# A hybrid attention step: the prompt attention in written order, larger groups of key blocks, and the sample recurrence on VectorE

## The chip, the cores and the metric

The kernel runs on one core of a Trainium2 chip. The metric is the device time of one execution in microseconds (us). A profile is one execution recorded by the hardware profiler. PE is TensorE's matmul, PEld its weight load, DVE is VectorE, ACT ScalarE, POOL GpSimd, SP SyncE, which issues most DMAs. An instruction's line (L1263) is a line of the kernel's source.

## What is computed

One layer of a hybrid decoder: 1024 prompt rows and 8 sample rows (one new row for each of 8 sequences with 1024 past rows) go through one projection, whose columns feed three groups of heads. All is float32. In the code that the change touches:

```python
def masked_softmax(s, mask): ...
# NSA group, 8 query heads on 2 KV heads, head_dim 64, a block of 128 queries at a time
s = jnp.einsum('qghd,cgd->qghc', qg, ck) * SCALE      # compressed blocks
p = masked_softmax(s, valid[:, None, None, :])
o_c = jnp.einsum('qghc,cgd->qghd', p.astype(cv.dtype), cv)
...
ss = jnp.einsum('qghd,qgnsd->qghns', qg, kg) * SCALE  # selected blocks: 16 of 64 rows
...
s = jnp.einsum('qghd,kgd->qghk', qg, kw) * SCALE      # window of 512 rows
...
return g[..., 0:1] * o_c + g[..., 1:2] * o_s + g[..., 2:3] * o_w
...
# RWKV group, one step of the recurrence; the sample rows make one such step
sa = jnp.einsum('bhvk,bhk->bhv', s, -kk_t)
s = s * w_t[:, :, None, :] + sa[..., None] * b_t[:, :, None, :] + v_t[..., None] * k_t[:, :, None, :]
return s, jnp.einsum('bhvk,bhk->bhv', s, r_t)
...
# memory group: 4 heads, softmax over 256 memory rows
s = jnp.einsum('bthd,bmhd->bhtm', q, mkv[:, :, 0]) * SCALE
...
cat = jnp.concatenate([o_nsa.reshape(b, t, NSA_W) * jax.nn.silu(z_nsa),
                       o_rw * jax.nn.silu(z_rw),
                       o_mem.reshape(b, t, MEM_W) * jax.nn.silu(z_mem)], axis=-1)
return cat @ w_out
```

With 1024 prompt rows there are 16 blocks of 64, so the 16 selected ones are all of a query's past.

## The kernel before

The program has three phases. Up to about 545 us come the projections and the prompt's RWKV scan; from 545 to about 915 us the prompt attention (`phase2`); then the sample's attention and the output projection. The change lies in `phase2` and in what runs beside it.

`phase2` walks 8 tiles of 128 queries from the last (i = 7) to the first (i = 0). A tile has four units (i, g, hp): KV head g and a pair hp of query heads. A unit has two branches: b = 0 the selected keys (i + 1 blocks of 128), b = 1 the window (at most five blocks). For each unit:

- `attn_scores` makes the scores p_s in PSUM. Keys are held as a high and a low part, so each stretch of keys is two matmuls (kh, L1263, and kl, L1264), and each masked block of 128 gets a third, a bf16 matmul of an identity with a mask (L1266), right behind its kl. A reduction on DVE gives the row maximum nm (L1279 in tiles 7 to 4, L1288 in 3 to 0), ScalarE takes the exponential (L1280, L1290), DVE makes the gate divided by the sum (fac, L1291 and L1292), and the probabilities p are scaled by it: the selected branch on DVE (L1296), the window on GpSimd (L1298). There are two score buffers.
- `attn_out` transposes p in blocks of 128x128 on PE (`pt_copy`, p_pT, L1236) into one of three PSUM banks, which ScalarE (L1240) and DVE (L1242) copy out in turn, and multiplies the values by the transposed blocks (p_o, L1320), 64 columns of the array a head. It does so in groups of four key blocks, with the next group's transposes written ahead of a group's p_o. The compressed branch comes last (cvk, L1323), then the product with the gate's SiLU into cat (L1325).

The scores of a unit are written LAG = 2 units ahead of its `attn_out`, in pieces between the groups. Beside them two chains of side tasks advance: `tile_tasks` (the next tile's queries in `q_stack`, the compressed branch in `attn_cmp`, the RWKV output in `attn_rwkv`, the memory heads in `attn_mem`) and `sample_tasks` (`sample_setup` with the norms of the sample's queries and keys, its memory and window attention, `sample_rwkv` with the recurrence, and the first gather of cache pages, L1660). How many of their steps run at each group is set by the table RATE, two numbers a tile. Within these, a scheduler orders the instructions of each engine.

`sample_rwkv` keeps the state as 128 partitions x 1024 (16 rows of 64) and makes its step with seven products or sums of 128x1024 on GpSimd (L1932 to L1940), with two reductions on DVE.

`attn_mem` takes the four heads at once: eight matmuls (L1337, L1338) into p_sm of 128x1024, one reduction (L1339), four exponentials (L1341), one product (L1343), eight transposes, sixteen products p_om and the product into cat (L1360).

## Time and profile before

| | us |
|---|---|
| median of 3 runs (1100.33 to 1103.5) | 1102.4 |
| the profiled execution | 1101.94 |
| its span in the trace | 1100.2 |
| PE busy | 1021.0 (93%) |
| DVE busy | 719.2 (65%) |
| ACT busy | 480.6 (44%) |
| POOL busy | 127.7 (12%) |

Shares of the whole span average over stages with different limits. The span is read by stretches: in each the busy time of an engine stands beside the length, and the granted clock shows whether TensorE ran at its upper level (2.4 GHz, 1.00) or partly at the lower one (1.2 GHz, 0.50).

### The profile page before, as it was taken

The page shows a single profiled execution, that of the slowest core. Times are in us where ns is not written, and L with a number is a line of the kernel's source. Part 1 is how long each engine was busy: PE and PEld are TensorE (multiplying, and loading weights), DVE is VectorE, ACT ScalarE, POOL GpSimd, SP SyncE. Part 2 cuts the span into 40 slices and gives each one's busy share as a digit, 9 for nine tenths or more (in the row PEclk, how much of TensorE's full clock was granted, in tenths as well). Part 3 has the DMA queues.
Part 4 walks back from the last instruction along what each step waited for, and adds up shares of the span by engine and source line. Part 5 has one row for each costly group of instructions (what it writes and reads, how often), then busy time and mean ns, then how long its engine had stood idle before and what let it go on. Part 6 is the DMA issues. An engine that isn't in the chain of part 4 may idle for free.

```text
span 1100.2 us, 27501 instructions
## 1 busy us (share of the span) xinstructions
PE 1021.0 (93%) x11419; PEld 830.8 (76%) x11419; DVE 719.2 (65%) x2065; ACT 480.6 (44%) x1056; POOL 127.7 (12%) x161
## 2 busy tenths in 40 slices
PE   6999999889999999999989979999998687999998
PEld 5998788678877787878767767777776576778676
DVE  7667488346925982734488985757788766575562
ACT  7553233324422433234266556665665355425320
POOL 1000000000000000000032231121326511101000
PEclk9999999999999999999999999999999699999999
DMA  8323113213311172361460034322100226526321
GB/s 258 98 56 88 43 44 111 61 41 86 88 51 32 44 183 65 90 179 41 128 195 21 25 117 130 101 59 71 34 4 14 99 57 227 199 88 239 116 77 60
DMA packets 124034, 102.25 MB, mean 93 GB/s; under 512 B 33455, under 2 KB 109646, under 8 KB 121734
## 3 DMA queue, kind: packets, MB, share of 16 engines
q1 hardware_dynamic: 119846, 82.50, 25.9%
q0 software_dynamic: 2304, 16.78, 4.5%
q8 instruction: 90, 1.47, 0.6%
q10 hardware_dynamic: 1760, 1.21, 0.4%
q14 instruction: 34, 0.28, 0.1%
HBM read 81.88 MB, written 22.78 MB: 95 GB/s over the span
## 4 chain that ended last, share of the span: by engine, by line
PE 68%; DVE 18%; DMA 5%; ACT 4%; issue 3%; POOL 1%; SPq 0%; DVEq 0%; ACTq 0%; POOLq 0%
PE p_pr L83 16%; PE p_pr L257 7%; PE p_pT L1236 6%; PE p_o L1320 5%; PE p_out L1996 5%; PE p_s L1263 3%; DMA wor<-in_w_out_dram 2%; PE p_it L83 2%; PE p_s L1264 2%; PE p_hid L958 2%; PE p_z L83 1%; DVE wlo L245 1%; PE p_iy L83 1%; DMA xg<-in_cache_nsa_dram,idx 1%; DVE nm L1279 1%
## 5 line engine op out<-in xcount | busy, mean ns | idle before, releaser
L83 PE MATMUL p_pr<-h,whi 128*128 128x512 f32 (+5 forms) x928 | 233.2, 343 | 0.0
L83 PEld LDWEIGHTS p_pr<-h,whi 128*128 128x128 f32 (+1 forms) x928 | 146.6, 185 | 18.0 <-issue 3.0
L83 PE MATMUL p_pr<-h,wlo 128*128 128x512 f32 (+5 forms) x464 | 152.7, 329 | 0.1
L83 PEld LDWEIGHTS p_pr<-h,wlo 128*128 128x128 f32 (+1 forms) x464 | 85.5, 184 | 9.7
L1263 PE MATMUL p_s<-kh,qs 128*128 128x512 f32 (+3 forms) x192 | 77.4, 404 | 13.4 <-ACT p L1280 8.2
L257 PE MATMUL p_pr<-h,whi 128*128 128x256 f32 (+2 forms) x416 | 87.8, 307 | 0.4 <-ACT whi L244 0.4
L1236 PE MATMUL p_pT<-ident,p 128*128 128x128 f32 x528 | 77.0, 288 | 9.3 <-DVE cat L1360 5.5
L1320 PE MATMUL p_o<-pt,vs 128*64 128x128 f32 x1056 | 84.9, 287 | 0.7 <-DVE cat L1325 0.6
L1298 POOL TENSOR_TENSOR p<-p,fac 128x640 f32<-128x640 f32 (+4 forms) x64 | 62.9, 1003 | 168.6 <-DVE fac L1292 105.7
L1236 PEld LDWEIGHTS p_pT<-ident,p 128*128 128x128 f32 x528 | 60.5, 146 | 20.9 <-issue 6.6
L1320 PEld LDWEIGHTS p_o<-pt,vs 128*64 128x64 f32 x1056 | 61.7, 140 | 15.8 <-issue 12.4
L245 DVE TENSOR_TENSOR wlo<-wraw,whi 128x1024 fp32r<-128x1024 f32 (+1 forms) x35 | 41.8, 1198 | 44.2 <-ACT whi L244 43.6
L1280 ACT ACTIVATE p<-p_s,nm 128x640 f32<-128x640 f32 (+3 forms) x64 | 55.8, 872 | 31.9 <-DVE nm L1279 28.1
L257 PEld LDWEIGHTS p_pr<-h,whi 128*128 128x128 f32 x416 | 66.7, 191 | 3.7 <-ACT whi L244 0.8
L1279 DVE TENSOR_REDUCE nm<-p_s 128x1 f32<-128x640 f32 (+3 forms) x64 | 58.4, 918 | 15.6 <-PE p_s L1266 15.4
L1264 PE MATMUL p_s<-kl,qs 128*128 128x512 f32 (+3 forms) x192 | 65.1, 344 | 0.0
L257 PE MATMUL p_pr<-h,wlo 128*128 128x256 f32 (+2 forms) x208 | 63.0, 305 | 0.0
L1242 DVE COPY pt<-p_pT 128x512 f32<-128x512 f32 (+1 forms) x72 | 47.8, 663 | 20.7 <-PE p_pT L1236 19.3
L1240 ACT ACTIVATE pt<-p_pT 128x512 f32<-128x512 f32 (+1 forms) x72 | 42.4, 591 | 41.9 <-PE p_pT L1236 37.5
L244 ACT ACTIVATE whi<-wraw 128x1024 fp32r<-128x1024 f32 (+1 forms) x35 | 36.3, 1037 | 49.9 <-PE p_pr L83 35.9
L1263 PEld LDWEIGHTS p_s<-kh,qs 128*128 128x128 f32 x192 | 37.6, 196 | 23.0 <-ACT p L1280 9.6
L1996 PE MATMUL p_out<-wol,chi 128*128 128x512 f32 x128 | 51.6, 403 | 1.7 <-DVE wol L1986 1.7
(528 smaller groups left out, 2186.4 us busy)
## 6 DMA issues: line engine op xcount, KB each, us to landing
wraw<-in_w_in_dram SPq DMA_DIRECT2D x34, 512.0 KB
x<-in_x_prompt_dram SPq DMA_DIRECT2D x8, 512.0 KB
z_d<-zt SPq DMA_DIRECT2D x16, 256.0 KB
cat<-z_d SPq DMA_DIRECT2D x8, 512.0 KB
wor<-in_w_out_dram SPq DMA_DIRECT2D x16, 256.0 KB
xres<-in_x_prompt_dram SPq DMA_DIRECT2D x16, 256.0 KB
out_dram<-xres SPq DMA_DIRECT2D x16, 256.0 KB
out_dram<-in_cache_win_dram SPq DMA_DIRECT2D x8, 511.0 KB
```

The lines of the kernel that those rows point to most:

```text
L83: self.last = getattr(self.engine, op)(*a, **k)
L245: nc.vector.tensor_tensor(lo[:, :, :n], raw[:, :, :n], hi[:, :, :n].bitcast(F32), op=OP.subtract)
L257: self.last_mm = self.pe.matmul(ps[:m, :b - a], w[:, k, :m], h[k][:, a:b], start=(k == 0 and i == 0), stop=(k == 7 and i == 2))
L1236: nc.tensor.transpose(ps[:, j, :], src(j), self.ident[:])
L1242: nc.vector.tensor_copy(pt[:, :n], ps[:, :n])
L1263: PE.matmul(ps, q, self.kh[u][:, 2 * b + g, o:o + w], start=True, stop=False)
L1264: PE.matmul(ps, q, self.kl[u][:, 2 * b + g, o:o + w], start=False, stop=not masks)
L1279: V.tensor_reduce(nm[:, h, b:b + 1], ps[:, c0:n1], axis=AX.X, op=OP.max, negate=True)
L1280: A.activation(Ps[h, b][:, :n1 - c0], ps[:, c0:n1], AF.Exp, bias=nm[:, h, b:b + 1], accum_out=sm[:, h, b:b + 1])
L1298: nc.gpsimd.tensor_tensor(x, x, bc(f[:, h, b:b + 1], x.shape), op=OP.mult)
L1320: PE.matmul(po[h * 64:h * 64 + 64], self.vs[k // 4][:, k % 4, b, g], pts[m // 2][:, 2 * (m % 2) + h], start=(n == 0 and m == 0), stop=False)
L1996: nc.tensor.matmul(po[:rows], c[:, k, :rows], w[:], start=(k == 0 and j == 0), stop=(k == 7 and j == 2))
```

## The change

All of PE's instructions of `phase2` go through a helper, `self.te = InOrder(...)`, that ties each to the one before, so that PE's order is the written one. (In the changed program all of these have the helper's line, L85.) The helper also adds up an estimated clock of PE's time. Further:

- The groups have up to eight key blocks: tiles 3 to 0 and no others have one group a unit; tile 7 has 8 + 5, tile 6 6 + 6, tile 5 6 + 5, tile 4 6 + 4. A new function, `attn_turn`, holds the transposes. The next group's (or next unit's) transposes come first, then the scores of the unit two ahead, then the p_o of this group.
- The masks of two neighbouring score stretches or heads stand together behind both.
- There are three chains of side tasks (queries and compressed branch; RWKV output and memory; sample). Each step names a time, and the chain goes on where the estimated clock has passed it, at most by START and RATE. `sample_setup` starts at once, and no longer behind the queries of tile 6; the recurrence starts at unit 16 at the earliest.
- The window's scaling in tiles 3 to 0 is on ScalarE in place of GpSimd.
- The seven products of the recurrence, and seven of 8x256 after it, are on DVE.
- `attn_mem` works in two halves of two heads; its products p_om are put off to the next `attn_out`, for tile 0 behind the last.
- The transposed blocks have eight buffers in place of four, the probabilities four in place of six.

```diff
-PTB = 4
+PTB = 8
...
-RATE = {7: (0.5, 0.4), 6: (0.9, 0.8), 5: (0.7, 0.7), 4: (0.7, 0.2), 3: (0.9, 0.9), 2: (1.4, 1), 1: (1.6, 1.1), 0: (2.3, 1.0)}
+RATE = {i: (0.6, 0.6, 1) if i > 3 else (1, 1, 1) for i in range(8)}
+START = (1.0, 0.0, 0.5)
...
-    def matmul(self, *a, **k):
-        return self._do("matmul", *a, **k)
+    def matmul(self, out, w, x, **k):
+        n = math.prod(x.shape[1:])
+        if out.shape[0] != self.rows:
+            self.rows = out.shape[0]
+            self.clock += 0.09
+        us = max(n, 256) * 4.6e-4 if x.dtype != F32 else max(n, 64) * 1.7e-3
+        self.clock += us * self.rows / 128
+        return self._do("matmul", out, w, x, **k)
...
-            for k, (o, m) in enumerate(masks):
-                PE.matmul(ps[:, o:o + 128], self.identb[:], self.bmask[:, m, :], start=False, stop=(k == len(masks) - 1))
+            return [(ps[:, o:o + 128], m, k == len(masks) - 1) for k, (o, m) in enumerate(masks)]
+
+        def add(masks):
+            for ps, m, stop in masks:
+                PE.matmul(ps, self.identb[:], self.bmask[:, m, :], start=False, stop=stop)
...
+                elif not split:
+                    A.activation(x, x, AF.Copy, scale=f[:, h, b:b + 1])
                 else:
                     nc.gpsimd.tensor_tensor(x, x, bc(f[:, h, b:b + 1], x.shape), op=OP.mult)
...
+    def attn_turn(self, i, Ps, n, m):
+
+        blocks = self.blocks(i)[n:m]
         w0 = max(0, 128 * (i - 4))
...
+        out = []
+        for j in range(0, len(blocks), 2):
+            src = [Ps[h, b][:, (k * 128 - b * w0):(k * 128 - b * w0) + 128] for b, k in blocks[j:j + 2] for h in range(2)]
+            out.append(self.pt_copy(lambda j: src[j], "b", len(src)))
+        return out
...
+    def attn_out(self, i, g, hp, pts, n, m):
+
+        PE = self.te
+        blocks = self.blocks(i)
+        if n == 0:
+            self.po = self.pO.tile([128, 128], F32, name="p_o", tag="o")
+        po = self.po
+        while self.tail:
+            self.tail.pop()()
...
     def sample_tasks(self):
+        yield from self.sample_setup()
         while ("q", 6) not in self.done:
-            yield
-        yield from self.sample_setup()
+            yield 1.0
...
+                total = len(self.blocks(i))
+                size = total if total <= 8 else -(-total // 4) * 2
+                groups += [(n, a, min(a + size, total)) for a in range(0, total, size)]
...
+            def slot():
+                for j in (2, 1, 0):
+                    spent[j] = min(spent[j] + rate[j], 3.0)
+                    while spent[j] >= 1 and self.te.clock >= ready[j]:
+                        step(j)
...
+                later = turn(*groups[j + 1]) if j + 1 < len(groups) else None
+                slot()
+                for _ in range(-(-pieces // left)):
+                    next(nxt, None)
+                    pieces -= 1
+                    slot()
...
+                self.attn_out(i, g, hp, pts, a, b)
+                slot()
+                pts = later
...
-        G.tensor_tensor(t, S, kb(0), op=OP.mult)
-        G.tensor_tensor(S, S, kb(4), op=OP.mult)
-        G.tensor_tensor(t2, vb(vv), kb(2), op=OP.mult)
-        G.tensor_tensor(S, S, t2, op=OP.add)
-        yield from wait(3)
+        V.tensor_tensor(t, S, kb(0), op=OP.mult)
+        yield 1.0
+        V.tensor_tensor(S, S, kb(4), op=OP.mult)
+        yield 1.0
         V.tensor_reduce(sa, t, axis=AX.X, op=OP.add)
```

PE's order in tile 5, before: p_o in groups of four blocks, transposes, and a mask behind each pair of key matmuls (vs are the values, kh and kl the keys, qs the queries, identb and bmask the masks).

```order
L1320 MATMUL p_o<-pt,vs_6938 64x128 x8
L1236 MATMUL p_pT<-ident,p 128x128 x6
L1263 MATMUL p_s<-kh_6936,qs 128x384
L1264 MATMUL p_s<-kl_6937,qs 128x384
L1266 LDWEIGHTS identb
L1266 MATMUL p_s<-bmask,identb 128x128
L1263 MATMUL p_s<-kh_6939,qs 128x256
L1264 MATMUL p_s<-kl_6940,qs 128x256
L1266 LDWEIGHTS identb
L1266 MATMUL p_s<-bmask,identb 128x128
```

The same place after, a whole group's p_o (12 halves), a side step (p_q), the next group's transposes and two score stretches with both masks at their end:

```order
L85 MATMUL p_o<-pt,vs_6938 64x128 x8
L85 MATMUL p_o<-pt,vs_6941 64x128 x4
L85 MATMUL p_q<-ident,qhl 128x128 x4
L85 MATMUL p_pT<-ident,p 128x128 x12
L85 MATMUL p_s<-kh_6936,qs 128x512
L85 MATMUL p_s<-kl_6937,qs 128x512
L85 MATMUL p_s<-kh_6939,qs 128x128
L85 MATMUL p_s<-kl_6940,qs 128x128
L85 LDWEIGHTS identb
L85 MATMUL p_s<-bmask,identb 128x128
L85 LDWEIGHTS identb
L85 MATMUL p_s<-bmask,identb 128x128
```

What moved: the runs of one kind are longer, and the two masks are neighbours.

GpSimd's order in tile 2, before: the window's scalings (p) and the products of the recurrence (rw_a), then the gather (xg) and a subtraction of the next queries (qhl).

```order
L1298 TENSOR_TENSOR p<-p,fac 128x384 x2
L1932 TENSOR_TENSOR rw_a_10987<-rw_a_10987,rw_a_10988 128x1024
L1298 TENSOR_TENSOR p<-p,fac 128x384 x2
L1933 TENSOR_TENSOR rw_a_10987<-rw_a_10987,rw_a_10988 128x1024
L1934 TENSOR_TENSOR rw_a_10988<-rw_a_10988 128x1024
L1935 TENSOR_TENSOR rw_a_10987<-rw_a_10987,rw_a_10988 128x1024
L1938 TENSOR_TENSOR rw_a_10987<-rw_a_10988 128x1024
L1939 TENSOR_TENSOR rw_a_10987<-rw_a_10987 128x1024
L1940 TENSOR_TENSOR rw_a_10987<-rw_a_10987,rw_a_10988 128x1024
L1298 TENSOR_TENSOR p<-p,fac 128x384 x2
L1660 DMA xg<-in_cache_nsa_dram,idx 128x2048
L1172 TENSOR_TENSOR qhl<-q,qhl 128x4x64
```

After, the products (L2016 and L2018 here, and L2022 the reduction) stand on DVE, one or two at a time between the steps of the softmaxes (nm the maxima, fac the gates, L1307 the selected branch's scaling, pmem the memory heads):

```order
L1362 TENSOR_REDUCE nm_m<-p_sm 128x2
L1307 TENSOR_SCALAR p<-p,fac 128x384 x2
L1303 RECIPROCAL fac<-fac 128x2
L2016 TENSOR_TENSOR rw_a_10760<-rw_a_10760 128x1024
L1365 RECIPROCAL sm_m<-sm_m 128x2
L2018 TENSOR_TENSOR rw_a_10760<-rw_a_10760,rw_a_10761 128x1024
L1366 TENSOR_TENSOR pmem<-pmem,sm_m 128x512
L1252 COPY pt<-p_pT 128x512
L1299 TENSOR_REDUCE nm<-p_s 128x2 x2
L2022 TENSOR_REDUCE rw_a_10761<-rw_a_10760 128x16
L1302 SCALAR_TENSOR_TENSOR fac<-sm,gates 128x2
L1344 TENSOR_TENSOR cat_11540<-cat_11540,p_o 128x128
```

What moved: nothing of the recurrence is left on GpSimd, and DVE does it between other work.

PE's order in tile 1, before: the p_o of a unit, the transposes of the unit after it, whose scores are a whole unit old, then the scores of the one after that.

```order
L1320 MATMUL p_o<-pt,vs_6938 64x128 x8
L1323 MATMUL p_o<-pt,cvk 64x128 x2
L1236 MATMUL p_pT<-ident,p 128x128 x8
L1263 MATMUL p_s<-kh_6936,qs 128x256
L1264 MATMUL p_s<-kl_6937,qs 128x256
L1266 LDWEIGHTS identb
L1266 MATMUL p_s<-bmask,identb 128x128
```

After, at the end of the same tile:

```order
L85 MATMUL p_s<-kh_6936,qs 128x256
L85 MATMUL p_s<-kl_6937,qs 128x256
L85 MATMUL p_s<-kh_6936,qs 128x256
L85 MATMUL p_s<-kl_6937,qs 128x256
L85 LDWEIGHTS identb
L85 MATMUL p_s<-bmask,identb 128x128
L85 LDWEIGHTS identb
L85 MATMUL p_s<-bmask,identb 128x128
L85 MATMUL p_sy<-ident,rw_a_10762 128x8 x2
L85 MATMUL p_o<-pt,vs_6938 64x128 x8
L85 MATMUL p_o<-pt,cvk 64x128 x2
L85 MATMUL p_pT<-ident,p 128x128 x8
```

What moved: the eight transposes now stand right behind a p_o that itself stands right behind the scores (the four rows of kh and kl) whose probabilities they turn.

## Rows read from the trace of the kernel before

**Rows 1.** The page: busy time and share by engine; the granted clock in 40 slices, tenths

```profile
PE 1021.0 (93%) x11419; PEld 830.8 (76%) x11419; DVE 719.2 (65%) x2065; ACT 480.6 (44%) x1056; POOL 127.7 (12%) x161
...
PEclk9999999999999999999999999999999699999999
```

**Rows 2.** Stretches: length, busy us of PE, PEld, DVE, ACT, POOL, clock, DMA, GB/s

```profile
545.00:600.00 55.00, 50.59 (x411) 37.80 (x412) 42.36 (x83) 34.31 (x69) 14.27 (x14) 0.97 0.44 131
600.00:640.00 40.00, 36.85 (x324) 28.54 (x322) 39.02 (x140) 24.27 (x56) 11.07 (x14) 1.00 0.13 41
600.00:660.00 60.00, 52.55 (x433) 41.09 (x432) 54.42 (x178) 33.18 (x74) 16.26 (x18) 0.97 0.21 65
780.00:800.00 20.00, 19.89 (x181) 15.13 (x179) 16.22 (x35) 12.17 (x30) 5.63 (x7) 1.00 0.09 28
840.00:860.00 20.00, 10.70 (x92) 8.15 (x91) 17.48 (x24) 8.39 (x27) 18.40 (x11) 0.86 0.07 28
860.00:880.00 20.00, 16.89 (x120) 13.54 (x119) 14.96 (x49) 8.79 (x27) 7.84 (x12) 0.71 0.32 108
```

**Rows 3.** Timeline of POOL: start, length, instruction; idle before and its releaser

```profile
842.49 2.37 POOL L1933 TENSOR_TENSOR rw_a<-rw_a,rw_a 128x1024 f32<-128x1024 f32 x1
...
856.87 1.61 POOL L1298 TENSOR_TENSOR p<-p,fac 128x384 f32<-128x384 f32 x2
```

**Rows 4.** Timeline of PE, behind those

```profile
858.55 1.97 PE L1236 MATMUL p_pT<-ident,p 128*128 128x128 f32 x8 [5.47 <-DVE cat L1360]
...
873.24 1.12 PE L1236 MATMUL p_pT<-ident,pcq 128*128 128x128 f32 x4 [1.75 <-DVE pcq L1217]
```

**Rows 5.** Waits of PE from 545 to 920: total us, times, longest

```profile
PE p_s L1263 <- ACT p L1280: 8.2, 7, 2.4
```

**Rows 6.** Timeline of PE in tile 7

```profile
609.73 0.28 PE L1337 MATMUL p_sm<-mkh,qs 128*128 128x256 f32 x1
609.85 0.28 PE L1338 MATMUL p_sm<-mkl,qs 128*128 128x256 f32 x1
610.06 1.09 PE L1320 MATMUL p_o<-pt,vs 128*64 128x128 f32 x16
611.08 0.44 PE L1236 MATMUL p_pT<-ident,p 128*128 128x128 f32 x2
...
611.60 0.23 PE L1266 MATMUL p_s<-bmask,identb 128*128 128x128 bf16 x1
611.64 0.42 PE L1263 MATMUL p_s<-kh,qs 128*128 128x384 f32 x1
611.90 0.33 PE L1264 MATMUL p_s<-kl,qs 128*128 128x384 f32 x1
612.08 0.23 PE L1266 MATMUL p_s<-bmask,identb 128*128 128x128 bf16 x1
612.24 1.31 PE L1320 MATMUL p_o<-pt,vs 128*64 128x128 f32 x20
...
613.70 0.33 PE L1236 MATMUL p_pT<-ident,p 128*128 128x128 f32 x1
```

**Rows 7.** Timeline of DVE

```profile
839.42 0.14 DVE L1291 SCALAR_TENSOR_TENSOR fac<-sm,gates 128x2 f32<-128x2 f32 x1
...
843.92 0.96 DVE L1288 TENSOR_REDUCE nm<-p_s 128x2 f32<-128x768 f32 x1 [0.29 <-PE p_s L1266]
844.80 1.22 DVE L1343 TENSOR_TENSOR pmem<-pmem,sm_m 128x1024 f32<-128x1024 f32 x1
...
847.99 2.24 DVE L1291 SCALAR_TENSOR_TENSOR fac<-sm,gates 128x2 f32<-128x2 f32 x1
```

**Rows 8.** Stretch with tile rq_t alone: length, busy us of DVE, clock, DMA, GB/s

```profile
600.00:640.00 40.00, 8.73 (x43) 1.00 0.13 41
```

**Rows 9.** Timeline of ACT

```profile
842.54 0.61 ACT L1240 ACTIVATE pt<-p_pT 128x512 f32<-128x512 f32 x1
843.02 0.60 ACT L1290 ACTIVATE p<-p_s,nm 128x384 f32<-128x384 f32 x1
```

More of the change, by code (lines that the diff above doesn't have):

```diff
@@ L49, in bc, with wait @@
     return ap.to_broadcast(shape)
-def wait(n):
-    for _ in range(n):
-        yield
+def wait(us):
+    yield us
 def weave(*gens):
@@ L79, in __init__ @@
         self.tc, self.engine, self.last = tc, engine, last
+        self.clock, self.rows = 0.0, 128
     def _do(self, op, *a, **k):
+        if self.last is None:
+            self.last = getattr(self.engine, op)(*a, **k)
+            return self.last
         with self.tc.issue_after(self.last.ins):
@@ new lines, in attn_turn, with blocks @@
+        out = []
[3 more added lines that the diff above has]
+        return out
+    def blocks(self, i):
+        return [(0, k) for k in range(i + 1)] + [(1, k) for k in range(max(0, i - 4), i + 1)]
+    def attn_out(self, i, g, hp, pts, n, m):
[6 more added lines that the diff above has]
+            self.tail.pop()()
+        for j, (b, k) in enumerate(blocks[n:m]):
+            for h in range(2):
+                PE.matmul(po[h * 64:h * 64 + 64], self.vs[k // 4][:, k % 4, b, g], pts[j // 2][:, 2 * (j % 2) + h],
+                          start=(n + j == 0), stop=False)
+        if m == len(blocks):
+            for h in range(2):
+                PE.matmul(po[h * 64:h * 64 + 64], self.cvk[:, g], self.pcT[i][:, 2 * hp + h], start=False, stop=True)
+            cat = self.cat[i][:, 2 * g + hp, :]
+            self.nc.vector.tensor_tensor(cat, cat, po[:], op=OP.mult)
@@ new lines, in attn_mem, with query_tasks @@
+        yield 1.0
+        self.tail.append(close)
+        while self.tail:
+            yield 1.0
+    def query_tasks(self):
+        yield from self.attn_cmp(7)
+        self.done.add(("cmp", 7))
+        for i in range(6, -1, -1):
+            while i < 6 and (self.unit < 4 * (5 - i) + 2 or ("mem", i + 2) not in self.done):
+                yield 1.0
+            if i == 6:
+                yield from weave(self.q_stack(6), self.mem_keys())
+                self.done.add("memory")
+            else:
+                yield from self.q_stack(i)
+            self.done.add(("q", i))
+            yield from self.attn_cmp(i)
+            self.done.add(("cmp", i))
@@ L1363, in tile_tasks @@
     def tile_tasks(self):
         for i in range(7, -1, -1):
[L1365 to L1374 removed]
+            while self.unit < 4 * (7 - i) or "memory" not in self.done:
+                yield 1.0
@@ L1446, in phase2 @@
-            for _ in chain(main, side):
-                pass
+            groups = []
+            for n, (i, _, _) in enumerate(units):
+                total = len(self.blocks(i))
+                size = total if total <= 8 else -(-total // 4) * 2
+                groups += [(n, a, min(a + size, total)) for a in range(0, total, size)]
+            P = [{} for _ in units]
+            self.done, self.tail, self.unit = set(), [], 0
+            gens = self.query_tasks(), self.tile_tasks(), self.sample_tasks()
@@ new lines, in turn @@
+            def turn(n, a, b):
+                return self.attn_turn(units[n][0], P[n], a, b)
+            for _ in chain(*(self.attn_scores(*units[n], P[n]) for n in range(LAG))):
+                slot()
+            pts = turn(*groups[0])
+            for j, (n, a, b) in enumerate(groups):
+                i, g, hp = units[n]
+                self.unit = n
+                if a == 0:
+                    nxt, pieces = iter(()), 0
+                    left = sum(1 for m, _, _ in groups if m == n)
+                    if (g, hp) == (0, 0):
+                        rate = RATE[i]
+                        until(0, ("cmp", i))
+                        if i == 4:
+                            until(2, "win")
+                        if i < 7:
+                            self.load_z(i)
+                    if n + LAG < len(units):
+                        ahead = units[n + LAG]
+                        if ahead[0] < 7:
+                            until(0, ("q", ahead[0]))
+                        nxt = self.attn_scores(*ahead, P[n + LAG])
+                        pieces = 4 if ahead[0] >= 4 else 2
+                later = turn(*groups[j + 1]) if j + 1 < len(groups) else None
[4 more added lines that the diff above has]
+                    slot()
+                left -= 1
+                if not left:
+                    for _ in nxt:
+                        pass
+                self.attn_out(i, g, hp, pts, a, b)
+                slot()
+                pts = later
@@ L1448, in phase2 @@
+            while min(ready) < 1e6:
+                for k in range(3):
+                    step(k)
+                while self.tail:
+                    self.tail.pop()()
+            self.te = nc.tensor
             self.kctx.close()
@@ L1910, in sample_rwkv @@
         V.tensor_copy(VEC[:, 5], v)
-        yield from wait(2)
+        yield from wait(5.0)
         for b0 in range(3):
```

257 lines of the change are left out of this document (106 added, 151 removed).

## The prediction

> **What bounds the kernel now.** I read the page's busy line and clock strip first [rows 1]: TensorE (PE) is busy 1021.0 of a span of 1100.2 us, so any gain must come from PE's own instructions taking less, or from the few stretches where PE stands. The strip of granted clock is at 9 but for one slice in tenths of 6, four fifths of the way along. Then the table by stretch [rows 2]: the prompt attention (545 to 915 us) is where the change lies. In 780 to 800 us PE is busy 19.89 of 20: dense. In 840 to 860 it is busy 10.70 and in 860 to 880 16.89, with mean clocks of 0.86 and 0.71. So that stage has 9.3 + 3.1 = 12.4 us of idle PE, and then runs partly at the lower of the clock's two levels. In 600 to 660 PE lacks 7.4 of 60 us and in 545 to 600 4.4 of 55.
>
> Who makes PE wait there? In 840 to 860 it is GpSimd (18.40 of 20 busy). Its queue holds seven products of 128x1024 of the sample recurrence, one every 2.3 us or so, and behind the last stands a pair of window scalings at 856.87 [rows 3]. The transposes that need those start at 858.55 after 5.47 us of idle PE, and then take 0.24 each [rows 4]; the view names a VectorE instruction as releaser, but the time is that of the scaling. In the first tiles the largest wait is that of score matmuls for ScalarE's exponentials to free a score buffer: 8.2 us in 7 waits, the longest 2.4 [rows 5]. VectorE is busy 39.02 of the 40 us from 600 to 640 [rows 2].
>
> The profiled execution took 1101.94 us, the span 1100.2; the sum is made against 1101.94, which lies 0.5 under the median of 1102.4.
>
> **The change, part by part.**
>
> (a) Fewer changes of array shape. An output matmul (p_o) uses half the array's columns, everything else in the loop all of them. Going by the order of instructions, from the first prompt scores to the last p_o neighbouring PE instructions differ in shape 233 times before and 131 times after: 102 fewer. The price, from starts [rows 6]: 16 halves take 1.02 us to the next start (610.06 to 611.08), 20 and the 4 of cvk behind them take 1.46 (612.24 to 613.70), so a pair costs 0.11 and the visit 1.02 - 8 x 0.11 = 0.14 beyond its pairs. Entering costs too: 609.85 to 610.06 is 0.21, where 609.73 to 609.85 of the same matmul kind is 0.12, so 0.09. A visit of two changes is 0.23, one change 0.12. 102 x 0.12 = -12. If only the 0.14 is real, 0.07 each: -7; if a mask that precedes p_o hides nothing of the entry (0.16 at 612.08 against 0.04 at 611.60, so 0.12), 0.13 each: -13. All of it is on PE, and counts in dense stretches; I take -12.
>
> (b) Masks in pairs. A mask itself takes 0.04 (611.60 to 611.64), but the key matmul of 384 columns behind it takes 0.26 where the same one behind another of its kind takes 0.18 [rows 6]. So a mask costs about 0.12, of which 0.08 is the change to and from bf16. There are 128, and after the change all stand in 64 pairs. A pair has no row. If two cost as one and a bare 0.04, each pair saves 0.08: -5. If nothing of the change of type is saved, 0; if the second is wholly free, 64 x 0.12 = -8. I take 0.06 a pair, -4, nearest to the one row that shows the return.
>
> (c) The recurrence leaves GpSimd. Removed: the wait of 5.47 and what surrounds it. Of the 12.4 us of idle in 840 to 880, 1.75 before 873.24 belongs to the compressed branch and stays [rows 4], so about 10.6 goes. The lower clock also goes if PE stays busy: means of 0.86 and 0.71 are, with half speed at the lower level, 2 x (0.14 + 0.29) x 20 = 17 us of it [rows 2], behind the two idle times; PE was busy for some 12 of them, an estimate from 27.6 of 40, and would do that work in 6. 10.6 + 6 = 16.6. Added to VectorE: seven products by 1.22 us, the row of a product of that size [rows 7], 8.5, and some 2 for seven small ones. On VectorE they stand between the steps of the softmax. But VectorE was held up by GpSimd: the gate factor of 128x2 takes 0.14 at 839.42 and 2.24 at 847.99, under GpSimd's products [rows 7]; summed over 800 to 880 such excess is about 12 us, an estimate from instructions of one form. So VectorE's load there stays level. Of the gain I keep 14, for products that still get in the way of one step each. Bounds: 5 (only the named wait) and 18. The gather that stood behind the products on GpSimd's queue starts earlier, and nobody waits for it before the next phase.
>
> The Trainium skill, "SBUF — State Buffer", section "SBUF: two separate sides", says that VectorE and GpSimd share a pair of SBUF ports as an exclusive lock, held for a whole instruction. The trace agrees (2.24 us against 0.14); by that rule the moved products give back what they take and the sum stands, and without it VectorE would have 10 us more in these tiles and the sum would be 1098.
>
> (d) The front. The sample's set-up now starts at once. Its norms on VectorE (43 instructions, 8.73 us of 600 to 640 in one tile alone [rows 8], with those of the keys some 15, an estimate) fall into the first two units, where VectorE has 12.6 us to spare in 55 [rows 2]; they leave 600 to 640, where it had 1.0. Its loads go on SP's queue earlier, at 0.44 of DMA use in 545 to 600 [rows 2]. The larger groups spread the score pieces differently, and the side steps are started by an estimate of PE's time instead of a table. I take -3 of the 11.8 us of idle in 545 to 660; bounds -8 (all score waits [rows 5] gone) and +15 (the set-up all on the path).
>
> (e) One group per unit in tiles 3 to 0. Before, a whole unit stood between a unit's scores and its transposes. Now the transposes of unit n+2 follow right behind p_o of unit n, which follow the scores of n+2. In tile 2 the softmax of the window branch after its last score is: reduce 0.96 [rows 7], two exponentials 0.60 each [rows 9], factor and reciprocal 0.14 each [rows 7], one to two scalings on ScalarE at about 0.6 (nearest row: the copy of 128x512, 0.61 [rows 9]), 3.1 to 3.7. The cover: p_o 1.46 [rows 6], six transposes of the selected branch at half the 0.24 of rows 4, a side step of some 0.5: 2.6. So 0.5 to 1.1 shows, with queueing on ScalarE about 1.0, near the mean of the waits of rows 5 (8.2/7 = 1.2). 16 units: +16. Bounds: 0 (side steps always stand between) and +38 (the longest of rows 5, 2.4, each time). The 32 window scalings of these tiles leave GpSimd's queue (1.61 for a pair [rows 3]) for ScalarE, which is 8.39 and 8.79 busy of 20 there [rows 2], so has room; their length is in this chain.
>
> (f) The memory attention of tile 0 closes behind the last p_o, so its copies and two products stand bare: +3 (0 to +5), from two reduces, copies and exponentials at 0.5 to 0.6 each [rows 9], partly beside sample steps. More buffers for transposed blocks (8 for 4) cost nothing.
>
> **Sum:** -12 - 4 - 14 - 3 + 16 + 3 = -14, so 1101.94 - 14 = 1088.
>
> **The rivals.** *The chain is hidden.* If the side steps fill each gap of (e), and the score waits all go, 1088 - 16 - 5 = 1067. For it: in tiles 3 and 2 the order has steps of the memory branch, the next queries and the sample between the units; against: such steps run out towards tile 0.
>
> *The chain is bare (slower).* In tiles 3 to 0 the recurrence's products on VectorE, 1.22 each, stand between a reduce and its factor, and every unit shows 2.4 us, not 1.0: 1088 - 16 + 38 = 1110. It decides from (1102 - 1072)/16 = 1.9 us a unit on; the row of 2.4 [rows 5] says that such waits occur, the mean of 1.2 that they are not the rule.
>
> *VectorE is full in the first tile.* The set-up's 15 us delay the first reduces: +15 in place of -3, 1106. The 12.6 us to spare speak against it, and that they aren't where they are needed speaks for it.
>
> *The order does nothing.* If PE waits wherever it gets ahead, the fewer changes of shape and paired masks just lengthen waits: 1088 + 16 = 1104. Dense rows such as 780 to 800 [rows 2] speak against it.
>
> **How the numbers follow.** Forecast 0.52, by its own terms 1077 to 1098; hidden chain 0.15; bare chain 0.15; VectorE full 0.09; order does nothing 0.09. The range of 8 in 10 is 1066 to 1107: it leaves out the far end of the hidden chain (0.06) and most of the bare one (0.13). 0.3%, 3.3 us, is about what a measurement can tell from no change: faster means under 1098.6, slower over 1105.2. Faster: 0.51 + 0.15 + 0.05 from the edges of the others = 0.71. Within: 0.11 (half of the last two and edges). Slower: 0.18.
>
> **What would show it.** (a, b) In a dense tile (5 or 4) the time from one tile's last cat to the next falls by 2 to 3 us with PE busy as before. (c) No p_pT wait over 2 us and a clock of 1.00 where the recurrence runs, factors back at 0.14. (d) VectorE below full in 600 to 640. (e) PE waits of about 1 us for p from ScalarE ahead of transposes, once a unit, from tile 3 on. (f) a few us of idle behind the last p_o. The forecast is wrong if (e) shows near 0 or over 2 a unit, or if the first two units stretch by over 10 us.

## The result

The changed kernel takes 1111.53 us (median of 6 runs, 1109.94 to 1115.6) against 1102.76 for the kernel before (6 runs, 1100.33 to 1103.54): a ratio of 1.009, interval 1.0067 to 1.0113. It is slower by 9 us where 14 less were forecast. The profiled execution of it took 1115.6 us, the longest of the six, and has a span of 1113.7 us.

The page of the changed kernel, its busy times and its strip of the clock, which answer to [rows 1]:

```profile
PE 1014.7 (91%) x11419; PEld 835.2 (75%) x11419; DVE 721.6 (65%) x2111; ACT 498.4 (45%) x1088; POOL 84.8 (8%) x115
...
PEclk9999899999999999999998899999999998999999
```

PE is busy 6 us less than before and the span is 13.5 us longer: what was saved came back as idle time, and more. The deep notch of the clock is gone, and shallow ones stand in its place. The same stretches as in [rows 2] (length, busy time of PE, PEld, DVE, ACT, POOL, clock, DMA, GB/s):

```profile
545.00:600.00 55.00, 41.68 (x297) 30.91 (x296) 49.56 (x165) 30.48 (x64) 13.34 (x16) 0.95 0.40 123
600.00:640.00 40.00, 33.34 (x273) 26.17 (x272) 27.46 (x73) 19.55 (x46) 7.49 (x8) 0.82 0.29 93
...
780.00:800.00 20.00, 19.90 (x201) 15.95 (x199) 13.82 (x30) 13.15 (x31) 4.62 (x5) 1.00 0.09 25
...
840.00:860.00 20.00, 15.76 (x144) 12.58 (x143) 18.98 (x40) 10.83 (x30) 0.00 (x0) 0.92 0.07 15
860.00:880.00 20.00, 16.75 (x164) 12.99 (x163) 16.38 (x44) 14.98 (x44) 2.81 (x3) 0.99 0.37 134
```

In 840 to 880 us PE is busy 32.5 us where it was 27.6, so 4.9 of the 12.4 us of the hole beside GpSimd's chain are filled. In 545 to 640 us it is busy 75.0 of 95, where it was 87.4. (The prompt attention begins 4.7 us later here, at 549.8, after a first phase with the same instructions, so 5 us of that are no change in it.)

To take such shifts out, I measure from the first prompt score on, and split the stretch up to the end of the last product of p_o into cat (the loop) in three: idle (gaps between matmuls in the timeline), loss to the lower clock (half of PE's busy time where the granted clock was at its lower level), and the rest, dense time. The tail is the time from there to the sample's first p_xt. All are worked out from the timelines of the profiled executions, in us. The ratio is that of a kernel's times to those of the kernel before on the same chip; that one took 1099.8 to 1103.1 us (medians) on the chips used, so ratios are surer to compare than times.

| kernel | ratio to before, interval | loop | idle | lower clock | dense | tail |
|---|---|---|---|---|---|---|
| before | 1 | 368.9 | 33.2 | 10.7 | 325.0 | 0.4 |
| changed | 1.009, 1.0067 to 1.0113 | 369.2 | 48.3 | 17.2 | 303.7 | 8.0 |
| e1 set-up later | 1.003, 1.0007 to 1.0053 | 367.3 | 46.3 | 17.1 | 304.0 | 6.8 |
| e2 transposes later | 0.9951, 0.9921 to 0.998 | 360.6 | 42.7 | 17.8 | 300.1 | 7.4 |
| e3 masks apart | 1.0066, 1.004 to 1.0092 | 369.0 | 47.0 | 14.0 | 308.0 | 8.0 |
| e4 groups of 4 | 1.0005, 0.9974 to 1.0037 | 360.7 | 44.0 | 10.9 | 305.9 | 6.8 |
| e5 memory earlier | 1.009, 1.0057 to 1.0122 | 374.3 | 49.3 | 20.4 | 304.6 | 1.8 |
| e6 recurrence on GpSimd | 1.0131, 1.0079 to 1.0182 | 373.4 | 49.9 | 20.8 | 302.8 | 6.8 |
| e7 before, recurrence on VectorE | 0.9987, 0.9963 to 1.0011 | 365.4 | 30.6 | 10.0 | 324.8 | 0.4 |
| e8 window scaling on GpSimd | 1.0156, 1.0117 to 1.0195 | 381.4 | 53.2 | 24.9 | 303.3 | 6.8 |
| e10 untied | 0.9926, 0.9897 to 0.9955 | 354.8 | 24.6 | 11.2 | 319.0 | 4.8 |
| e11 untied, e2 | 0.9874, 0.9835 to 0.9914 | 349.8 | 23.0 | 7.8 | 319.0 | 3.4 |
| e13 untied, e2, e5 | 0.9834, 0.9786 to 0.9882 | 349.0 | 21.1 | 8.4 | 319.5 | 1.4 |
| e14 untied, groups of 4 | 0.9804, 0.9754 to 0.9854 | 338.7 | 20.8 | 2.7 | 315.1 | 4.8 |
| e16 e14, recurrence on GpSimd | 0.9811, 0.9766 to 0.9856 | 342.8 | 21.3 | 3.8 | 317.7 | 4.8 |
| e17 e14, tiles 1 and 0 late, e5 | 0.9736, 0.9706 to 0.9766 | 338.6 | 16.5 | 3.4 | 318.8 | 0.5 |
| e19 e14, set-up later | 0.9857, 0.9816 to 0.9898 | 346.7 | 23.1 | 7.9 | 315.7 | 4.8 |

Loop and tail are of one execution each, the ratios of 4 to 10. Taken against the changed kernel, the differences of loop and tail together agree with those of the ratios (times 1102) within 4 us in all rows but one: for e2 the ratios give 15.3 us less and the trace 9.2.

For the change: dense -21.3, idle +15.1, lower clock +6.5, loop +0.3. The tail adds 7.6, of which 3.7 is dense work that left the loop. So 17.6 us of PE time was truly saved, and 17.6 of idle and 8.0 of lower clock (loop and tail) were paid for it: +8.0. With 1.0 more in the last phase that is +9.0.

**Where the idle time is.** First the front. PE's timeline of the changed kernel in tile 7:

```profile
590.30 0.23 PE L85 MATMUL p_s<-bmask,identb 128*128 128x128 bf16 x1
...
592.36 0.66 PE L85 MATMUL p_k<-ident,kd 128*128 128x128 f32 x4
592.86 1.04 PE L85 MATMUL p_pT<-ident,p 128*128 128x128 f32 x8
597.48 1.97 PE L85 MATMUL p_pT<-ident,p 128*128 128x128 f32 x8 [3.59 <-DVE mkl L1071]
...
604.70 0.41 PE L85 MATMUL p_qs<-ident,s_in 8*128 8x8 f32 x4
608.59 0.38 PE L85 MATMUL p_qs<-ident,nr_y 8*128 8x8 f32 x2 [3.47 <-DMA mxv<-in_cache_mem_dram]
```

and VectorE's there:

```profile
593.62 0.27 DVE L359 TENSOR_TENSOR nr_o<-nr_o,nr_sq 8x128 f32<-8x128 f32 x1
...
593.89 1.21 DVE L1291 TENSOR_REDUCE nm<-p_s 128x1 f32<-128x1024 f32 x1
...
596.75 0.67 DVE L1071 TENSOR_TENSOR mkl<-p_k,mkh 128x512 fp32r<-128x512 f32 x1
...
605.76 1.38 DVE L343 TENSOR_TENSOR nr_y<-s_in,rq_r 8x256 f32<-8x256 f32 x1
607.17 1.36 DVE L344 TENSOR_TENSOR nr_y<-nr_y,gains 8x256 f32<-8x256 f32 x1
```

The side step p_k at 592.36 took one of the three PSUM banks that the transposes use as well. The bank comes free with mkl, which VectorE does only at 596.75, behind norms of the set-up (nr_o is one) and two reductions of scores that were done at 590.5 (the first is shown). The transposes at 597.48 waited 3.59 us for it, and since PE's order is fixed, everything behind them did. At 604.70 the set-up's own transposes come up; the next two need nr_y, which ends at 608.53 (the releaser that the view names, a DMA, is not the one). Nothing else may run on PE for 3.47 us, and the clock of 600 to 640 is 0.82.

Then tiles 3 to 0. The waits of PE for the transposes' operands there (799 to 919 us), of ScalarE's and of VectorE's scaling:

```profile
PE p_pT L85 <- ACT p L1309: 10.6, 14, 2.1
...
PE p_pT L85 <- DVE p L1307: 3.2, 5, 1.2
```

Two such places on PE in tile 2, and VectorE under the second:

```profile
855.43 0.33 PE L85 MATMUL p_pT<-ident,p 128*128 128x128 f32 x1 [1.61 <-ACT p L1309]
...
859.98 0.44 PE L85 MATMUL p_s<-bmask,identb 128*128 128x128 bf16 x2
860.34 1.53 PE L85 MATMUL p_o<-pt,vs 128*64 128x128 f32 x24
...
863.92 1.56 PE L85 MATMUL p_pT<-ident,p 128*128 128x128 f32 x7 [1.16 <-DVE p L1307]
```

```profile
861.33 1.21 DVE L2012 TENSOR_TENSOR rw_a<-rw_a,rw_a 128x1024 f32<-128x1024 f32 x1
862.46 0.15 DVE L1302 SCALAR_TENSOR_TENSOR fac<-sm,gates 128x2 f32<-128x2 f32 x1
...
863.46 0.73 DVE L1307 TENSOR_SCALAR p<-p,fac 128x384 f32<-128x384 f32 x2
```

The unit's scores end at 860.4, p_o and a memory step follow, and the transposes of this very unit wait for p; a product of the recurrence (861.33) stands ahead of fac, which is back at 0.15 us (0.14 in [rows 7]).

Last the tail, on PE:

```profile
918.30 0.39 PE L85 MATMUL p_o<-pt,cvk 128*64 128x128 f32 x4
918.62 0.39 PE L85 MATMUL p_sm<-mkh,qs 128*128 128x256 f32 x1
...
922.20 1.08 PE L85 MATMUL p_pTm<-ident,pmem 128*128 128x128 f32 x4 [2.38 <-DVE pmem L1366]
...
924.92 1.41 PE L85 MATMUL p_om<-ptm,mv 128*64 128x128 f32 x16
...
927.07 1.09 PE L1799 MATMUL p_xt<-ident,x 128*128 128x128 f32 x8 [0.49 <-DVE x L1786]
```

Behind the last p_o stand the last scores of the memory heads (p_sm), a wait of 2.38 us for their probabilities, the transposes and p_om.

### The profile page after: what moved, and what is told of

Read it like the earlier page. It is cut to its first block, busy times and chain, and to the rows that moved or that the text cites. A ratio compares the mean times of both kernels' runs of the same rounds, so it can differ in the third digit from the quotient of the medians.

```text
span 1113.7 us, 27464 instructions
## 1 busy us (share of the span) xinstructions
PE 1014.7 (91%) x11419; PEld 835.2 (75%) x11419; DVE 721.6 (65%) x2111; ACT 498.4 (45%) x1088; POOL 84.8 (8%) x115
## 3 DMA queue, kind: packets, MB, share of 16 engines
q1 hardware_dynamic: 119846, 82.50, 25.6%
## 4 chain that ended last, share of the span: by engine, by line
PE 63%; DVE 19%; DMA 8%; ACT 5%; issue 3%; SPq 1%; POOL 0%; ACTq 0%; DVEq 0%; POOLq 0%
PE p_pr L85 17%; PE p_pr L267 7%; PE p_out L2073 6%; PE p_s L85 5%; PE p_pT L85 4%; PE p_o L85 3%; DMA xg<-in_cache_nsa_dram,idx 3%; PE p_it L85 2%; DVE nm L1291 1%; PE p_hid L968 1%; PE p_z L85 1%; DVE pt L1252 1%; PE p_iy L85 1%; DMA wor<-in_w_out_dram 1%; ACT p L1301 1%
## 5 line engine op out<-in xcount | busy, mean ns | idle before, releaser
L85 PE MATMUL p_pr<-h,whi 128*128 128x512 f32 (+5 forms) x928 | 234.3, 344 | 0.0
L85 PEld LDWEIGHTS p_pr<-h,whi 128*128 128x128 f32 (+1 forms) x928 | 147.5, 186 | 18.1 <-issue 3.0
L85 PE MATMUL p_pr<-h,wlo 128*128 128x512 f32 (+5 forms) x464 | 153.5, 331 | 0.0
L85 PE MATMUL p_pT<-ident,p 128*128 128x128 f32 x528 | 78.5, 288 | 24.1 <-ACT p L1309 10.6
L85 PEld LDWEIGHTS p_pr<-h,wlo 128*128 128x128 f32 (+1 forms) x464 | 85.9, 185 | 9.7
L85 PEld LDWEIGHTS p_pT<-ident,p 128*128 128x128 f32 x528 | 60.4, 145 | 38.2 <-ACT p L1309 15.9
L85 PE MATMUL p_s<-kh,qs 128*128 128x512 f32 (+3 forms) x191 | 74.9, 399 | 12.1 <-ACT p L1292 8.0
L85 PE MATMUL p_o<-pt,vs 128*64 128x128 f32 x1056 | 69.1, 279 | 0.4 <-DVE cat L1344 0.4
L85 PE MATMUL p_s<-kl,qs 128*128 128x512 f32 (+3 forms) x192 | 64.9, 354 | 0.0
L85 PEld LDWEIGHTS p_o<-pt,vs 128*64 128x64 f32 x1056 | 58.2, 139 | 5.5 <-issue 2.4
L1250 ACT ACTIVATE pt<-p_pT 128x512 f32<-128x512 f32 x72 | 42.5, 592 | 29.2 <-PE p_pT L85 29.0
L85 PEld LDWEIGHTS p_s<-kh,qs 128*128 128x128 f32 x191 | 39.3, 206 | 17.5 <-ACT p L1292 9.6
L2073 PE MATMUL p_out<-woh,chi 128*128 128x512 f32 x128 | 51.5, 402 | 0.0
```

The costliest lines, as they stand in the source:

```text
L85: self.last = getattr(self.engine, op)(*a, **k)
L1250: nc.scalar.activation(pt[:, :n], ps[:, :n], AF.Copy)
L2073: self.te.matmul(po[:rows], c[:, k, :rows], w[:], start=(k == 0 and j == 0), stop=(k == 7 and j == 2))
```

## The experiments

Several causes could have made the loss: the tie on PE (every late operand stops all that is behind it), VectorE and ScalarE simply being late, the set-up's place, or the group size. The experiments test these, and each term of the forecast by itself.

**e1.** `sample_setup` behind the queries of tile 6.

```diff
-        yield from self.sample_setup()
         while ("q", 6) not in self.done:
             yield 1.0
+        yield from self.sample_setup()
```

> The changed kernel with one edit: the sample's set-up starts behind the queries of tile 6 again, as before the change. Theory: the set-up's small VectorE norms, queued between the first tile's reductions and scalings, make most of the 14 us of extra PE idle in tile 7 (20.3 against 5.9 us); then this gives 8 us back: about 1103, PE idle in tile 7 near 8 us. Rival: the loss in the first tile comes from the larger groups and the written order, and where the set-up stands does not matter: 1110 to 1112, idle in tile 7 still 15 us or more.

1104.84 us, near the theory's 1103 (6.6 us less than the changed kernel by the ratios), but not as expected: tile 7 is 15.6 us shorter (100.1 to 84.5) and tile 4 is 11.0 longer, as the sample's window must be done there. The first four tiles gain 1.9 us, the loop 1.9, loop and tail 3.1. In the loop the load moved, more than it went; where the rest of the 6.6 us comes from isn't shown.

**e2.** In tiles 3 to 0 the scores two units ahead are written first, and the next unit's transposes behind them.

```diff
-                later = turn(*groups[j + 1]) if j + 1 < len(groups) else None
-                slot()
+                if i >= 4:
+                    later = turn(*groups[j + 1]) if j + 1 < len(groups) else None
+                    slot()
...
                     for _ in nxt:
                         pass
+                if i < 4:
+                    later = turn(*groups[j + 1]) if j + 1 < len(groups) else None
+                    slot()
```

> The changed kernel with one edit: in tiles 3 to 0 the transposes of the next unit are written behind the scores of the unit two ahead in place of ahead of them, which puts a unit's scores between a softmax and its transposes. Theory: the bare softmax chain costs the waits of transposes for scalings seen there (10.6 us for ScalarE's, 3.2 for VectorE's): 10 us go, about 1101, and those waits fall under 3 us. Rival: these tiles are held by the load of VectorE and ScalarE, so the waits only move to the scores or the p_o: 1109 to 1113.

1096.7 us, the theory and more. Tiles 3 to 0 take 108.8 us in place of 119.6, and the wait in these tiles is

```profile
PE p_pT L85 <- ACT p L1309: 2.1, 2, 1.5
```

where it was 10.6. That is what the place of the transposes cost, the wait that term (e) priced: 10.8 us, of 16 forecast.

**e3.** Each mask right behind its key matmuls.

```diff
-            return [(ps[:, o:o + 128], m, k == len(masks) - 1) for k, (o, m) in enumerate(masks)]
+            add([(ps[:, o:o + 128], m, k == len(masks) - 1) for k, (o, m) in enumerate(masks)])
+            return []
```

> The changed kernel with each mask back behind its own key matmuls, nothing else. Theory: a pair of masks saves 0.06 us, so 64 pairs apart cost 4 us: dense PE time of the prompt attention (length less idle less time lost to the lower clock) rises from 304 to 308, the time to 1115. Rival: the pairs save nothing, 304 and 1111.

Dense time 308.0, as the theory said: 4.3 us for 64 pairs. But the time is 1108.2, by the intervals not to be told from the changed kernel's, and the loop is 369.0 long, since idle fell by 1.3 and the lower clock's loss by 3.2. So what the pairs save on PE doesn't show in the loop. Whether that is more than chance one trace each can't tell: the lower clock's loss in the first phase, whose instructions are the same in all these kernels, differs by 6.8 us between executions.

**e4.** `size = 4` for all groups.

> The changed kernel with groups of four key blocks in every tile, as before the change. Theory: shorter groups put another group's transposes and p_o between a softmax and its own transposes, so that 6 to 8 of the 21 us of idle PE in tiles 3 to 0 go; some 60 more changes of shape cost 7: about 1111. Rival: the idle stays and the changes of shape come on top: 1118.

1101.0 us, better than either said. 52 more changes of shape (175 against 123, counted to the last p_o in the timelines; term (a) counted the order of instructions) cost only 2.2 us of dense time; idle fell by 4.3 and the lower clock's loss by 6.3. Tile 7 is 6.5 us shorter and tile 3 is 3.6; tiles 3 to 0 together are 4.4 shorter.

**e5.** The memory attention of tiles 2 to 0 starts up to 3, 5 and 7 units ahead of its tile, with the RWKV output behind it and a pause of 1.0 in place of 4.0 between its halves.

```diff
-            while self.unit < 4 * (7 - i) or "memory" not in self.done:
+            while self.unit < 4 * (7 - i) - LEAD.get(i, 0) or "memory" not in self.done or (i < 7 and ("q", i) not in self.done):
...
+LEAD = {2: 3, 1: 5, 0: 7}
```

> The changed kernel with the memory attention of tiles 2 to 0 started earlier (before its tile begins; the RWKV output of those tiles behind it), so that tile 0's is nearly done at the last p_o. Theory: the 8.8 us between the last p_o and the sample's first p_xt (1.1 before the change) are the uncovered memory softmax at the lower clock: 6 us go, about 1105. Rival: its work and waits only move into tiles 1 and 0, which get as much longer: 1110 to 1112.

1110.25 us, the rival: the tail is 1.8 us in place of 8.0, and the loop 5.1 longer (tiles 2 and 0 are 5.9 and 4.7 longer, tile 1 is 5.0 shorter).

**e6.** The seven products back on GpSimd (`V.tensor_tensor` to `G.tensor_tensor`).

> The changed kernel with the seven products of 128x1024 of the recurrence back on GpSimd. Theory: as in the kernel before, where moving them took 3.5 us from the prompt attention of the profiled run, their place is worth little: 1112 to 1116. Rival: in the changed order VectorE has no room for them, and GpSimd, freed of the window's scalings, does them beside: 1105 or less. Second rival: the price of 14 us that was forecast: 1125.

1112.0 us, the first theory, by the intervals not to be told from the changed kernel's time; the loop is 4.2 us longer.

**e7.** The reverse in the kernel before (`G.tensor_tensor` to `V.tensor_tensor` for the seven).

> The kernel before with one edit: the seven products of 128x1024 of the sample's recurrence on VectorE in place of GpSimd. Theory: the chain on GpSimd costs the 12 us of idle PE and the slower clock of 840 to 880 us, and VectorE gets back in held-up instructions what the products add: 12 to 14 us less, about 1089. Rival: VectorE was held up only while PE waited anyway, so the products fill it and PE waits for its reductions: 1098 to 1102.

1099.99 us, ratio 0.9987, which can't be told from 1: the rival. In the trace the loop is 3.5 us shorter (tile 2 by 7.0, while tile 1 is 3.4 longer), and the two stretches read

```profile
840.00:860.00 20.00, 15.90 (x123) 12.58 (x121) 18.59 (x30) 9.04 (x27) 7.82 (x5) 0.83 0.07 22
860.00:880.00 20.00, 15.87 (x148) 12.60 (x149) 18.88 (x59) 9.67 (x31) 8.27 (x12) 1.00 0.35 122
```

GpSimd is out of the way, but VectorE is busy 18.6 and 18.9 of 20, where it was 17.48 and 14.96 [rows 2], and PE still idles 8.2 us there. Over the whole loop VectorE is busy 277.7 us in both kernels: the seven products came in, and as much held-up time went.

**e8.** The window's scaling of tiles 3 to 0 back on GpSimd (the `elif not split` branch left out).

> The changed kernel with the window's scaling of tiles 3 to 0 back on GpSimd. Theory: on ScalarE the scaling queues behind the next unit's exponentials and is part of the waits of transposes (10.6 us for these), GpSimd is idle there but takes twice as long for it: 0 to 3 us either way, 1109 to 1114. Rival: ScalarE's queue is what makes the chain long: 1104 or less.

1118.6 us, which neither said: the loop is 12.2 us longer. The waits of the transposes in these tiles are

```profile
PE p_pT L85 <- POOL p L1309: 17.7, 22, 2.4
```

where those for ScalarE's scaling were 10.6 in 14. A pair of 128x384 takes 1.11 us on ScalarE (854.78 in the changed kernel); on GpSimd it takes 1.61 at 835.78 and 2.45 at 855.31 and 867.32, where a product of 128x1024 runs on VectorE. So this part of the change, to which the prediction gave no gain of its own, was worth 7 us in the time.

**e10.** The written order stays, the tie goes.

```diff
-        if self.last is None:
+        if self.last is None or self.free:
...
             self.te = InOrder(tc, nc.tensor, None)
+            self.te.free = True
```

> The changed kernel with the same written order, but without the tie between one PE instruction of the prompt attention and the next, so that the scheduler may move others ahead (221 changes of shape in place of 123 up to the last p_o). Theory: in the written order one late operand stops everything behind it on PE, and most of the 15 us of idle that came in is this: idle falls from 48 to 36, dense time rises by 10: about 1110. Rival: the idle comes from VectorE and ScalarE being late for all of it: idle stays, 1120.

1093.1 us, 18 less than the changed kernel and more than the theory said: idle fell by 23.7 us (12 expected), the lower clock's loss by 6.0, while 98 more changes of shape (221 against 123) cost 15.3 of dense time. Where the tied kernel stood 3.47 us between the set-up's transposes of s_in and of nr_y, others now run (those of nr_y come at 607.25):

```profile
594.02 0.41 PE L82 MATMUL p_qs<-ident,s_in 8*128 8x8 f32 x4
594.36 0.44 PE L82 MATMUL p_yT<-ident,y_rw 128*128 128x128 f32 x2
```

At the place of p_k, where the tied kernel stood 3.59 us, PE still stands, a little less, now for a score buffer:

```profile
584.86 0.47 PE L82 MATMUL p_s<-kh,qs 128*128 128x128 f32 x1 [2.66 <-ACT p L1292]
```

In the first four tiles idle falls from 26.9 to 14.3 us, and the waits for scaled probabilities in tiles 3 to 0 are

```profile
PE p_pT L82 <- ACT p L1309: 1.2, 4, 0.4
PE p_pT L82 <- DVE p L1307: 1.0, 2, 0.7
```

**e11.** e10 with e2.

> The changed kernel without the tie on PE, and with the transposes of tiles 3 to 0 written behind the next scores. Theory: the two edits pay for the same waits (transposes that stand in front of a softmax that isn't done), so together they give little over the untied kernel's 1093: 1090 to 1094, prompt attention 352 to 355 us. Rival: they are independent, 18 and 12 us: 1081.

1087.7 us, between the two. The loop is 5.0 us shorter than e10's, where e2 alone gave 8.6: the two share part of their gain.

**e13.** e11 with e5.

> As the kernel with the tie gone and the later transposes, and the memory attention of tiles 2 to 0 started earlier. Theory: untied, PE has other work in tiles 1 and 0, so that here the tail shortens without these tiles getting longer: 4 us less than without, about 1088. Rival: as in the tied kernel the work only moves: 1092.

1082.0 us, the theory (4.4 us less than e11 by the ratios, though their intervals overlap). In the trace, tail and loop together are 2.8 us shorter than e11's; here tiles 3 to 0 don't get longer (106.7 against 107.0 us).

**e14.** e10 with e4.

> The changed kernel without the tie on PE and with groups of four key blocks. Theory: the scheduler now fills the gaps, so the larger groups are worth their fewer changes of shape: dense time rises by 2 to 7 us, idle stays at 25: 1095 to 1100. Rival: groups of four shorten idle as they did in the tied kernel (9 us in the time): 1086.

1077.8 us, the rival and beyond: 15 less than e10. The front is

```profile
545.00:600.00 55.00, 46.44 (x361) 32.61 (x360) 52.38 (x179) 33.00 (x72) 17.10 (x19) 1.00 0.35 105
600.00:640.00 40.00, 39.73 (x377) 30.85 (x374) 30.55 (x65) 27.29 (x62) 7.09 (x7) 1.00 0.44 138
```

with VectorE busier in 545 to 600 (52.38) than before (42.36) or in the changed kernel (49.56), and the clock at 1.00 throughout. Dense time is lower than e10's too (315.1), at about as many changes of shape (218). Why, these runs don't tell.

**e16, e17, e19** start from e14: the seven products on GpSimd; the transposes of tiles 1 and 0 late as in e2 (`i >= 2` for `i >= 4`) with e5; `sample_setup` as in e1.

> The changed kernel without the tie on PE and with groups of four (1078), and with the seven products of the recurrence back on GpSimd. Theory: the products on GpSimd hold up VectorE and the chain stands in the way of whole units, but only some 3.5 us of it ever showed on PE: 1080 to 1084, tile 2 some 4 us longer. Rival: with everything else out of the way the full price of the first reckoning shows, 12 to 14 us: 1091. Second rival: GpSimd is free now, VectorE is not: 1076 or less.

1080.2 us, within the theory's range, though by the ratios (0.9811 and 0.9804) it can't be told from e14. In the trace the loop is 4.1 us longer, tile 2 by 6.0.

> The changed kernel without the tie on PE and with groups of four; besides, in tiles 1 and 0 (one group a unit still) the transposes behind the next scores, and the memory attention of tiles 2 to 0 earlier. Theory: the 3 us that the earlier memory attention and the 5 us that the later transposes were worth in the untied kernel with large groups add up in part: 1073 to 1076. Rival: what is left in tiles 1 and 0 is VectorE's and ScalarE's load: 1078.

1073.7 us, the theory, and the lowest of all: 2.6% under the kernel before. In the trace the gain is the tail's, 0.5 us in place of 4.8; the loop is as long as e14's, with 3.7 us more dense time in it. What the later transposes add isn't shown apart.

> The changed kernel without the tie on PE and with groups of four, and with the sample's set-up behind the queries of tile 6 as before the change. Theory: where the set-up stands only shifts its load between tile 7 and tile 4, as in the tied kernel (tile 7 shorter by 16 us, tile 4 longer by 11): 1076 to 1080. Rival: with the tie gone tile 7's remaining 9 us of idle are the set-up's: 1070.

1085.7 us, neither: here the loop is 8.0 us longer with the later set-up, where in the tied kernel it was 1.9 shorter. By the ratios e19 takes 5.8 us more than e14, with intervals that overlap, so that the early set-up is a gain here is likely rather than shown.

## Why the prediction was wrong, step by step

**(a), (b) Fewer changes of shape, masks in pairs: right as a sum.** Forecast -16 on PE's own time, measured -17.6 of dense time (loop and tail). For the pairs, forecast -4, e3 showed 4.3. The price of one change, 0.12 by [rows 6], is not settled: e10 gives 15.3/98 = 0.16, e4 2.2/52 = 0.04, and both moved other work too.

**"All of it is on PE, and counts in dense stretches": the step that failed first.** PE's stretches did not stay dense. The prediction spoke of the written order only as what reduces changes of shape, and gave no price to the tie itself, that is to what PE would do whenever the next instruction in the written order is not ready. e10 puts it at 18 us: with the tie 48.3 us of idle and 17.2 of lower clock, without it 24.6 and 11.2. By the ratios the tie also costs 8.5 us in e2's order (e11 against e2) and 22 with groups of four (e14 against e4), each time clear of the intervals. What it costs hangs on the order: e2 keeps the tie, only writes the transposes of four tiles later, and takes 15 us less by itself; together the two give 24 (e11). I had argued the case as a rival, "the order does nothing", with a gain of 0, not with a loss behind it, and let [rows 2] speak against it: the dense 780 to 800 us of a kernel whose scheduler was free.

**(c) The recurrence: mis-sized.** Forecast -14, measured 3.5, 4.2 and 4.1 us of the loop (e7, e6, e16), in three different orders; in the times none of the three can be told from nothing, and e7's interval leaves a gain of 4 us at most. The hole in [rows 2, 4] was real, and so was the held-up VectorE (2.24 us for fac [rows 7], 0.15 after), and VectorE's load stayed level as forecast (277.7 us in the loop, e7). The step from there to PE failed: the 12.4 us of idle was not GpSimd's alone. The products must still be done; with them VectorE is busy 18.6 of 20 us, one stands ahead of a factor at 861.33, PE still idles 8.2 us (e7), and half of what tile 2 gains is lost in tile 1. I had counted all idle time of the stretch as one wait's. The lower bound of 5, "only the named wait", was the better reading. The Trainium skill, "SBUF — State Buffer", section "SBUF: two separate sides", has VectorE and GpSimd hold a shared pair of ports as an exclusive lock. The factors and the 277.7 us agree with it. That the 1098 worked out without the rule came nearer than 1088 speaks against the step from VectorE to PE, not against the lock.

**(d) The front: wrong in sign.** Forecast -3 of the idle; its sign came true, VectorE busy 27.46 of 40 us in 600 to 640, and yet in the first four tiles idle rose from 15.8 to 26.9 us and the lower clock's loss from 3.4 to 8.7, +16.4 together. That is the size that the rival "VectorE is full in the first tile" had (+15), but not quite its cause: e1 moved the set-up away and won 1.9 us in these tiles (6.6 in the time), the loop of e19 is longer by it, and with tie and large groups gone (e14) the set-up stands as early as ever and VectorE is fuller, with 10.5 us of idle and none of the lower clock. The tie alone is 12.6 of the idle (26.9 to 14.3, e10). No exponential from 549 to 920 us waits for a buffer of probabilities, so four of these in place of six aren't a cause. What made the front dear is seen in the rows at 592 to 608 us: side steps that hold a transposes' bank, or whose operand is late, in an order from which PE can't step aside. Of the two, e10 dissolves the second and hardly the first (3.59 to 2.66 us).

**(e) One group per unit: right in kind, 10.8 for 16.** The waits are where they were looked for, 10.6 us in 14 for ScalarE's scaling. The 10.8 is what e2 gets back by the order; e4, which undoes the groups themselves, gets 4.4 in these tiles. The working was off by a little: its rows add up to 3.0 to 3.7 of chain and 2.7 of cover, so 0.4 to 1.0 and not 0.5 to 1.1 was to show; e2 gives 0.7 a unit. The scaling on ScalarE was counted as part of this cost; e8 shows that GpSimd makes it dearer, by 12.2 us of loop.

**(f) The tail: about right.** It is 7.6 us longer, but 3.7 of that is work that left the loop and is counted there; 3.9 of idle and lower clock stand against 3 forecast. e5 shows that in the tied order moving this work wins nothing. With the tie gone loop and tail are 2.8 us shorter by it (e13), and the tail 4.3 (e17).

**The sum.** By measured sizes: -17.6 dense (-21.3 in the loop, of which 3.7 went to the tail as work), and 25.6 of idle and lower clock, make +8; with 1.0 in the last phase +9. The bare-chain rival named almost this time (1110), but by 2.4 us at each of 16 units, and e2 gave 0.7: its nearness is luck.

## What to carry to other kernels

Fixing one engine's order saves what changes of shape cost only if each operand is surely there in time. Before tying, list for every instruction in the written order who delivers it and who frees its buffer, side steps too; what a scheduler hides by stepping aside becomes bare. An idle stretch with one named wait is worth that wait at most, until it is known where the work behind the wait goes: ask what the engine that takes over will be late with. And a step that looks worthless or harmful in one order (the early set-up, the earlier memory attention) may be a gain in another, so that parts of a change are tested again when the largest fault is out.

## What was not expected of the hardware

The lower clock's loss was large where idle time was large, but not in proportion: 2.7 us in e14 with 20.8 of idle, 11.2 in e10 with 24.6, 10.9 in e4 with 44.0, 24.9 in e8 with 53.2. In these kernels it came to between 0.13 and 0.47 us for each idle us.

The first phase, the same instructions in all these kernels, ended between 540.6 (e2) and 549.8 us (the changed kernel) in the profiled executions. That alone is as large as the difference that was to be explained, and it is why loops are compared here and not spans. Much of it is the clock: in that phase the lower level cost 6.8 us in the changed kernel and in e7, which ended it last (549.8 and 548.4), and nothing in e2 and e13, which ended it first (540.6 and 541.0).
